# The context's Fourier mixing ahead of the experts, and the rest of layer 0's modulation right behind the router

## Chip, cores and metric

The kernel runs on one core of a Trainium2 chip. The metric is the device time of one execution, in microseconds (us). A measurement is the median of several executions.

## What is computed

Two transformer blocks, one behind the other, on 256 tokens of width 1024, all in float32. The first mixes tokens (two kinds of attention), attends to a memory of 256 rows, and has a mixture of 16 experts. The second has two layers that work on two streams: the latent `x` (what the first block gives) and a context of 256 rows, which doesn't depend on the first block. The part of the reference that the change touches:

```python
mod_c = jax.nn.silu(c_ctx) @ w_mod[l] + b_mod[l]      # and mod from c
sh1c, sc1c, ga1c, sh2c, sc2c, ga2c = jnp.split(mod_c, 6, axis=-1)
hc = modulate(rmsnorm(xc, g_norm1[l]), sh1c, sc1c)
pfc, mqc, mkc, mvc, moc, mgc, cqc, ckvc, krc = split_proj(hc @ w_in[l])
...
y_fc = fourier_mix(pfc)          # real part of a 2-d FFT per group of 64
y_mc = mlstm_output(hcf, hcb, moc, g_mlstm[l])
y_ac = merge_heads(softmax_attend(qn_c, qr_c, (ctx_keys,)))
xc = xc + ga1c * (jnp.concatenate([y_fc, y_mc, y_ac], axis=-1) @ w_out[l])
xc = xc + ga2c * sqrelu_mlp(modulate(rmsnorm(xc, g_norm2[l]), sh2c, sc2c), w_up[l], w_down[l])
```

The modulation vectors of a layer depend on `c`, `c_ctx` and `w_mod` alone, so they can be computed at any time before their use.

## The kernel before

**Products.** A float32 product is made from three products of rounded parts: each weight tile is loaded (`raw`), ACT casts its high part (`whi`, L330), DVE subtracts it from the tile (`wlo`, L331), and PE adds up hi x hi, lo x hi and hi x lo (L364 to L366, in `gemm_a`). Activations are split in the same way: `th`/`tl` for a norm's output, `x2h`/`x2l` for the mixed heads that the output projection of a layer takes in, `hh`/`hl` inside the MLP. `wload` does this, with buffers of their own for work in the foreground and in the background.

**Order.** The program is written as a chain of regions, each with a rank from a table (`RK`): first 10, context in 19, experts 20, context out 22, context mix 23, and so on. A scheduler lists each engine's instructions ahead of time: an instruction of lower rank goes first where it is ready by the scheduler's own model, and one of a higher rank fills in. The engines then take their rows strictly in that order. All weight loads are on SP's queue.

**Layers.** `Layer(l, s)` is one layer of the second block on a stream (s = 1: context). `norm1` is its first norm, `enter` makes keys, queries, values and gates, `gate_out` and `spectrum_in` two more input products, `recur` the mLSTM (L962 to L1020, scores and their weights, one step for each of four heads), `attend` the attention (L919 scores, L928 transposes of the weights, L932 the sum over values, L936/L937 its scale, L942 the transposes of the result), `fourier` the Fourier mixing: four products with a table `dft` (L889), a copy (`z`), and eight with `cn` and `sn` (L898, L899), a split into `x2h`/`x2l` for the first two of eight rows of the projection. `project` is the projection, `norm2` and `mlp` follow. A norm sums squares (L419), takes a root on POOL, makes a diagonal tile `dg` (L433 on DVE, L431 on ACT), spreads it with a product (L435), and then scales each of eight tiles (`nt`, L454; `tl`, L464). The latent's first norm in layer 0 folds in the first block's last norm: its sums are L616 to L627, it has two diagonal tiles and two L435, the second for the residual (L635).

**Modulation.** `w_mod` of both layers is done in 48 rounds (`mod_jobs`, three groups of eight rounds for each layer). A round loads two tiles of 512 KB (L526) into two buffers and runs four matmuls side by side (L538); each waits for both loads. After eight rounds a sum (`modulate_sum`, four products L554, then L555, and L561 where a gain is folded in) gives 16 columns of modulation. `modulation(l, f)` runs all that is still to do up to column group f; `spread(3, 0, 47)` lets `tick` give one step with every third weight load of the foreground. Before the change the main program spreads the rounds over the first block, and the rest of layer 0 comes with the weight loads of the latent's `enter`, or at the latest where `project` and `norm2` of the context ask for it.

**The branch.** Behind the experts the kernel tests whether a group of experts overflowed (`experts_over`, L1635). The order of each engine is cut there: rows ahead of the branch, and rows behind it.

**Main program around the change** (L1660 on): `mix_tokens`, the context's `context_in` (rank 19, background), `mix_memory` (memory attention, and the router at L1352 to L1359), `context_mix` (rank 23, background), then `experts`, `experts_over`, and the latent's layer 0.

```python
    def context_mix(L):
        L.recur()
        L.attend()
        L.fourier()
```

Of the kernel before, what the change touches and what calls it, by code (L numbers as in the profile page):

```python
# [222 lines left out]
def _body(ctx, tc, A, out):  # L223
# [343 lines left out]
    def pending(l, f):  # L567
        return "done" in part or mod_jobs and mod_jobs[0] <= (l, f // 16, KT - 1)

    def modulation_step():  # L570
        with background(True):
            if "done" in part:
                modulate_sum()
            else:
                modulate_round(*mod_jobs.pop(0))

    def modulation(l, f):

        while pending(l, f):
            modulation_step()  # L580

    def spread(every, l, f):

        pace[0], pace[1], pace[2] = every, (l, f), 0
# [520 lines left out]
    def load_ctx():  # L1105
        RES[1] = [slot(256, name="ctx") for _ in range(KT)]
        for k in range(KT):
            nc.sync.dma_start(RES[1][k], A["ctxT"][:, k, :])

    def context_in():  # L1110
        load_ctx()
        L = Layer(0, 1)
        L.norm1()
        L.enter()
        L.gate_out()
        L.spectrum_in()
        L.share()
        return L

    def context_mix(L):  # L1120
        L.recur()
        L.attend()
        L.fourier()

    def context_out(L):
        load_ctx()
# [486 lines left out]
    def experts(R):  # L1613
        U, SN, gate, _ = R
        ready = {}

        def prepare(q):
            O = dispatch(SN, q)
            ready[q] = gather(U, O), slot_gates(O, gate, q), [back(O, p) for p in range(2)]
        prepare(0)  # L1620
        for p in range(8):
            q = p // 2
            if q not in ready:
                prepare(q)
            us, W, OT = ready[q]
            j = p % 2
            pair_experts([u[:, j * 128:(j + 1) * 128] for u in us], W[:, j:j + 1], OT[j], p)
            if p % 2 == 0 and q < 3:
                prepare(q + 1)
# [33 lines left out]
    with region(RK["ctx"], True):  # L1663
        LC = context_in()
    with region(RK["first"]):
        XG = mix_memory()
    with region(RK["cmix"], True):
        context_mix(LC)
    with region(RK["moe"]):
        spread(0, 0, 0)  # L1670
        experts(XG)
        experts_over(XG)
        spread(3, 0, 47)
        L = Layer(0, 0)
# [17 lines left out]
    with region(RK["l1"]):  # L1692
        L = Layer(1, 0)
# [47 lines left out]
```

## Time and profile before

| | us |
|---|---|
| median of 3 runs | 1589.96 |
| lowest and highest | 1586.74 and 1597.65 |
| the profiled execution | 1601.72 |
| its span in the profile | 1599.6 |

The profile is of one execution. PE is TensorE, PEld its weight loads, DVE the vector engine, ACT the scalar engine, POOL GpSimd, SP the engine that issues the loads. Times count from the start of the span. A matmul on float32 data (Fourier, modulation, attention) appears as two records, the products of rounded parts as one. A row of a timeline names the line of the code, the operation, what it writes and reads, and in brackets how long the engine was idle before it and what it waited for.

### The profile page before, as it was taken

To read this page: it belongs to the slowest core of one execution; us is meant where nothing else is said; L and a number is where in the kernel's file an instruction comes from. 1 tells how busy PE (TensorE), PEld (TensorE's weight loads), DVE (VectorE), ACT (ScalarE), POOL (GpSimd) and SP (SyncE) were. 2 spreads that over 40 slices of the span, in tenths; PEclk is the share of its full clock that TensorE was granted. 3 is DMA by queue.
4 is the path that set the end of the run, shared out by engine and by line. 5 is a ranking of instruction groups with operands and counts; after the bars stand their busy time and mean duration, and the time that the engine had idled before them with its cause. 6 is when DMAs were issued, how large, how long until landed. Compare 5 with 4: busy or idle time off the path is not lost. (4 is left out here: it accounts for less than half of the span.)

```text
span 1599.6 us, 27409 instructions
## 1 busy us (share of the span) xinstructions
PE 1514.9 (95%) x10646; PEld 1298.3 (81%) x10646; DVE 911.7 (57%) x1937; ACT 711.2 (44%) x1530; POOL 30.2 (2%) x99
## 2 busy tenths in 40 slices
PE   6999999989999986999999999999999899999998
PEld 5669788867744445888998999999888677899998
DVE  5635466676633437675675434444776663576665
ACT  4435555444422234465554323233545445455555
POOL 0000000000000000000000000000000000000000
PEclk9869999999999997999999999999989998999999
DMA  7735554354678765432355422222356651245553
GB/s 245 255 132 186 183 184 171 136 211 158 219 252 295 277 236 186 159 120 69 102 197 217 146 92 95 91 95 95 123 172 247 215 202 43 102 145 176 187 183 119
DMA packets 91001, 268.65 MB, mean 168 GB/s; under 512 B 10224, under 2 KB 16368, under 8 KB 90864
## 3 DMA queue, kind: packets, MB, share of 16 engines
q1 hardware_dynamic: 90864, 266.83, 47.8%
q8 instruction: 86, 1.41, 0.3%
q14 instruction: 51, 0.42, 0.1%
HBM read 265.74 MB, written 1.05 MB: 167 GB/s over the span
## 5 line engine op out<-in xcount | busy, mean ns | idle before, releaser
L330 ACT CAST whi<-raw 128x512 fp32r<-128x512 f32 (+2 forms) x614 | 364.0, 602 | 449.3 <-PE ps L365 360.6
L331 DVE TENSOR_TENSOR wlo<-raw,whi 128x512 fp32r<-128x512 f32 (+2 forms) x614 | 404.4, 668 | 275.8 <-ACT whi L330 268.2
L364 PE MATMUL ps<-th,whi 128*128 128x256 f32 x1496 | 433.8, 291 | 4.4 <-ACT th L463 3.2
L366 PE MATMUL ps<-th,wlo 128*128 128x256 f32 x1496 | 427.7, 287 | 5.2 <-DVE wlo L331 5.2
L365 PE MATMUL ps<-tl,whi 128*128 128x256 f32 x1496 | 429.3, 289 | 0.1
L364 PEld LDWEIGHTS ps<-th,whi 128*128 128x128 f32 x1496 | 289.7, 194 | 21.4 <-ACT th L463 5.4
L366 PEld LDWEIGHTS ps<-th,wlo 128*128 128x128 f32 x1496 | 289.1, 194 | 9.5 <-DVE wlo L331 7.5
L365 PEld LDWEIGHTS ps<-tl,whi 128*128 128x128 f32 x1496 | 289.1, 194 | 7.9 <-issue 5.0
L364 PE MATMUL ps<-hh,whi 128*128 128x256 f32 x768 | 218.0, 284 | 2.1 <-ACT hh L474 1.0
L365 PE MATMUL ps<-hl,whi 128*128 128x256 f32 x768 | 217.0, 283 | 0.2 <-DVE hl L475 0.2
L366 PE MATMUL ps<-hh,wlo 128*128 128x256 f32 x768 | 216.9, 283 | 0.0
L364 PEld LDWEIGHTS ps<-hh,whi 128*128 128x128 f32 x768 | 145.2, 189 | 4.8 <-ACT hh L474 2.7
L365 PEld LDWEIGHTS ps<-hl,whi 128*128 128x128 f32 x768 | 144.3, 188 | 0.5 <-DVE hl L475 0.5
L366 PEld LDWEIGHTS ps<-hh,wlo 128*128 128x128 f32 x768 | 144.2, 188 | 0.3
L538 PE MATMUL mod<-raw,scT 128*32 128x512 f32 x320 | 67.1, 644 | 8.6 <-DMA raw<-in_wmod_dram 8.5
L1552 PE MATMUL ps<-raw,us 128*64 128x512 f32 x128 | 59.4, 601 | 1.0 <-DMA raw<-in_wgu_dram 0.9
L364 PE MATMUL ps<-x2h,whi 128*128 128x256 f32 x192 | 55.0, 286 | 0.5 <-ACT x2h L474 0.5
L366 PE MATMUL ps<-x2h,wlo 128*128 128x256 f32 x192 | 54.6, 284 | 0.4 <-DVE wlo L331 0.4
L365 PE MATMUL ps<-x2l,whi 128*128 128x256 f32 x192 | 54.6, 284 | 0.1
L1064 DVE SCALAR_TENSOR_TENSOR res<-ps,mod,res 128x256 f32<-128x256 f32 x80 | 35.1, 479 | 33.2 <-PE ps L366 33.1
L1094 DVE TENSOR_TENSOR rl<-rl 128x512 f32<-128x512 f32 x48 | 32.9, 686 | 34.5 <-ACT rl L1092 34.5
L395 PE MATMUL ps<-whi,th 128*128 128x512 f32 (+1 forms) x128 | 48.4, 382 | 0.1
(416 smaller groups left out, 2224.3 us busy)
## 6 DMA issues: line engine op xcount, KB each, us to landing
raw<-in_wmod_dram SPq DMA_DIRECT2D x80, 512.0 KB, 4.6
raw<-in_wup_dram SPq DMA_DIRECT2D x72, 512.0 KB, 3.2
raw<-in_wdn_dram SPq DMA_DIRECT2D x64, 512.0 KB, 3.2
raw<-in_wo_dram SPq DMA_DIRECT2D x32, 512.0 KB, 3.2
raw<-in_wgu_dram SPq DMA_DIRECT2D x32, 512.0 KB, 4.6
raw<-in_w2m_dram SPq DMA_DIRECT2D x29, 512.0 KB, 3.4
raw<-in_w2c_dram SPq DMA_DIRECT2D x21, 512.0 KB, 3.5
raw<-in_w1a_dram SPq DMA_DIRECT2D x16, 512.0 KB, 4.5
```

The lines of the kernel that those rows point to most:

```text
L330: nc.scalar.copy(hi, raw[:, p * m:p * m + m])
L331: nc.vector.tensor_sub(lo, raw[:, p * m:p * m + m], hi)
L364: mm(o, wh, xh, start=k == order[0] and not (both and j), stop=False)
L365: mm(o, wh, xl, start=False, stop=False)
L366: mm(o, wl, xh, start=False, stop=k == order[-1] and (not both or j == len(fs) - 1))
L395: mm(o, xh, wh, start=st, stop=False)
L538: m = mm(ps[32 * j:32 * j + 32, :], scT[:, k, :], W[j], start=k == 0, stop=k == KT - 1, tile_position=(0, 32 * j))
L1064: stt(self.res[f], ps[:, j * 256:(j + 1) * 256], self.mod[:, off + f, self.s:self.s + 1], self.res[f], op0=ALU.mult, op1=ALU.add)
L1094: tt(r_, r_, r_, op=ALU.mult)
L1552: mm(ps[64 * j:64 * j + 64, :], us[k][:, 64 * j:64 * j + 64], ws[j][kk], start=k == 0, stop=k == 7, tile_position=(0, 64 * j))
```

## The change

`fourier` of the context moves from `context_mix` (behind recurrence and attention, rank 23) into `context_in` (ahead of `share`, rank 19). And behind `mix_memory`, in the region of rank 10, the main program asks for all of layer 0's modulation.

```diff
@@ -1114,13 +1114,13 @@
         L.enter()
         L.gate_out()
         L.spectrum_in()
+        L.fourier()
         L.share()
         return L
 
     def context_mix(L):
         L.recur()
         L.attend()
-        L.fourier()
 
     def context_out(L):
         load_ctx()
@@ -1664,6 +1664,7 @@
         LC = context_in()
     with region(RK["first"]):
         XG = mix_memory()
+        modulation(0, 47)
     with region(RK["cmix"], True):
         context_mix(LC)
     with region(RK["moe"]):
```

PE, the first rows behind the branch. `ya` is the context's attention, `wq` the squares' weights of the latent's first norm, `mod` a round of modulation; L364 on `th` is the first product of the latent's layer. Before:

```order
L942 MATMUL ps<-cst,ya 128x128
L621 MATMUL ps<-wq,sq 128x2 x2
L942 MATMUL ps<-cst,ya 128x128
L621 MATMUL ps<-wq,sq 128x2 x2
L942 MATMUL ps<-cst,ya 128x128
L621 MATMUL ps<-wq,sq 128x2 x12
L942 MATMUL ps<-cst,ya 128x128 x2
L435 MATMUL ps<-dg,cst 128x256
L538 MATMUL mod<-raw,scT 32x512
L435 MATMUL ps<-dg,cst 128x256
L364 MATMUL ps<-th,whi 128x256
```

After the change:

```order
L621 MATMUL ps<-wq,sq 128x2 x16
L928 MATMUL ps<-cst,ae 128x128 x2
L932 MATMUL pa<-vm,apt 128x96 x2
L435 MATMUL ps<-dg,cst 128x256
L942 MATMUL ps<-cst,ya 128x128 x6
L364 MATMUL ps<-x2h,whi 128x256
L365 MATMUL ps<-x2l,whi 128x256
L366 MATMUL ps<-x2h,wlo 128x256
L364 MATMUL ps<-x2h,whi 128x256
```

The round has gone from behind the branch. The end of the context's attention (L928, L932) has come there from ahead of it, and 13 rows of the context's projection (L364 to L366 on `x2h`/`x2l`) stand between the two L435.

SP, ahead of the router: the weights of memory attention (`wxq`, `wxv`, `wxo`), of the context (`w2m`, `wuv`, `wuq`) and of the modulation (`wmod`). Before:

```order
L324 DMA raw<-in_wxq_dram 128x1024 x5
L324 DMA raw<-in_wxv_dram 128x1024 x2
L324 DMA raw<-in_wxq_dram 128x1024
L324 DMA raw<-in_w2m_dram 128x1024
L324 DMA raw<-in_wxq_dram 128x1024 x2
L324 DMA raw<-in_wxo_dram 128x1024 x5
L324 DMA raw<-in_w2m_dram 128x1024 x2
L810 DMA wuv<-in_wukv_dram 128x384
L836 DMA wuq<-in_wuq_dram 128x512 x2
L526 DMA raw<-in_wmod_dram 128x1024 x2
L324 DMA raw<-in_w2m_dram 128x1024
```

After the change:

```order
L324 DMA raw<-in_wxq_dram 128x1024 x4
L526 DMA raw<-in_wmod_dram 128x1024
L324 DMA raw<-in_wxq_dram 128x1024
L526 DMA raw<-in_wmod_dram 128x1024
L324 DMA raw<-in_wxv_dram 128x1024 x2
L526 DMA raw<-in_wmod_dram 128x1024
L324 DMA raw<-in_wxq_dram 128x1024 x3
L324 DMA raw<-in_wxo_dram 128x1024 x5
L526 DMA raw<-in_wmod_dram 128x1024
L324 DMA raw<-in_w2m_dram 128x1024 x2
L526 DMA raw<-in_wmod_dram 128x1024 x2
L324 DMA raw<-in_w2m_dram 128x1024
```

Loads of the modulation now stand singly between those of memory attention, from the queries' weights on.

PE, in the third step of the latent's recurrence. Before, the last three of ten rows of the context's projection stand ahead of the first product with `mw`:

```order
L366 MATMUL ps<-x2h,wlo 128x256
L364 MATMUL ps<-x2h,whi 128x256
L365 MATMUL ps<-x2l,whi 128x256
L366 MATMUL ps<-x2h,wlo 128x256
L998 MATMUL ps<-vr,mw 128x97
L364 MATMUL ps<-x2h,whi 128x256
L962 MATMUL ps<-qkc 128x256 x2
L968 MATMUL ps<-grr,selr 128x512
L970 LDWEIGHTS bfc
L970 MATMUL ps<-bfc 128x256
L998 MATMUL ps<-state,qx 128x97
```

After the change, at the same step:

```order
L968 MATMUL ps<-grr,selr 128x512
L970 LDWEIGHTS bfc
L970 MATMUL ps<-bfc 128x256
L419 MATMUL ps<-cst,sq 128x1 x4
L998 MATMUL ps<-vr,mw 128x97
L962 MATMUL ps<-qkc 128x256 x2
L968 MATMUL ps<-grr,selr 128x512
L970 LDWEIGHTS bfc
L970 MATMUL ps<-bfc 128x256
```

The rows of the projection are gone from there; the sum of the context's second norm (L419) has taken their place.

## Rows read from the trace of the kernel before

**Rows 1.** The page, part 1: busy us (share of the span) and instructions.

```profile
PE 1514.9 (95%) x10646; PEld 1298.3 (81%) x10646; DVE 911.7 (57%) x1937; ACT 711.2 (44%) x1530; POOL 30.2 (2%) x99
```

**Rows 2.** Stretches: length, busy PE, PEld, DVE, ACT, POOL, PEclk, DMA, GB/s.

```profile
300.00:592.00 292.00, 274.86 (x1660) 178.59 (x1662) 155.21 (x412) 101.63 (x261) 7.40 (x26) 0.98 0.67 233
440.00:560.00 120.00, 113.44 (x607) 58.41 (x607) 48.34 (x131) 30.00 (x92) 1.98 (x2) 0.99 0.78 275
595.00:615.00 20.00, 9.85 (x40) 8.27 (x41) 9.59 (x26) 9.36 (x23) 2.26 (x6) 0.50 0.56 197
617.00:629.00 12.00, 12.00 (x95) 11.82 (x95) 10.35 (x23) 6.40 (x12) 0.00 (x0) 0.93 0.28 95
629.00:639.00 10.00, 6.21 (x37) 4.55 (x35) 8.05 (x21) 5.97 (x12) 0.95 (x8) 0.84 0.61 209
639.00:643.00 4.00, 4.00 (x21) 3.92 (x20) 1.15 (x2) 0.62 (x1) 0.00 (x0) 0.54 0.22 85
643.00:665.00 22.00, 20.79 (x144) 18.48 (x144) 16.75 (x39) 10.33 (x25) 0.76 (x2) 1.00 0.47 156
680.00:740.00 60.00, 58.86 (x441) 53.14 (x440) 43.85 (x104) 36.76 (x100) 2.55 (x7) 1.00 0.29 100
740.00:770.00 30.00, 27.24 (x179) 24.23 (x178) 15.90 (x35) 16.04 (x36) 0.70 (x1) 0.94 0.16 53
```

**Rows 3.** PE behind the branch: start, us, instruction, [idle before <-releaser].

```profile
595.18 0.45 PE L942 MATMUL ps<-cst,ya 128*128 128x128 f32 x1 [2.37 <-PEq L1635]
...
614.65 1.91 PE L538 MATMUL mod<-raw,scT 128*32 128x512 f32 x2 [7.53 <-DMA raw<-in_wmod_dram]
...
616.56 1.19 PE L435 MATMUL ps<-dg,cst 128*128 128x256 f32 x2
```

**Rows 4.** Timeline of DVE in the first hole.

```profile
603.75 0.41 DVE L475 TENSOR_TENSOR x2l<-ps,x2h 128x256 fp32r<-128x256 f32 x1
...
609.33 0.68 DVE L331 TENSOR_TENSOR wlo<-raw,whi 128x512 fp32r<-128x512 f32 x1
...
616.13 0.28 DVE L433 TENSOR_SCALAR dg<-cst,rp 128x128 f32<-128x128 f32 x1
```

**Rows 5.** Timeline of PE in the second hole.

```profile
629.53 1.06 PE L538 MATMUL mod<-raw,scT 128*32 128x512 f32 x6
...
630.52 1.99 PE L889 MATMUL ps<-dft,pf 128*128 128x256 f32 x8
...
632.35 0.95 PE L554 MATMUL mod<-cst,mrow 128*128 128x8 f32 x8
...
638.07 1.22 PE L435 MATMUL ps<-dg,cst 128*128 128x256 f32 x2 [2.63 <-ACT dg L431]
```

**Rows 6.** Timeline of PE in the Fourier's second half.

```profile
652.00 0.59 PE L899 MATMUL ps<-sn,z 128*128 128x256 f32 x2
652.43 0.59 PE L898 MATMUL ps<-cn,z 128*128 128x256 f32 x2
```

**Rows 7.** PE by line, 300 to 592 us: busy, mean ns of one, idle.

```profile
L932 PE MATMUL pa<-vm,apt 128*128 128x96 f32 x32 | 5.3, 287 | 2.4 <-ACT apt L930 2.4
...
L928 PE MATMUL ps<-cst,ae 128*128 128x128 f32 x16 | 3.4, 297 | 0.0
```

**Rows 8.** Waits of PE, 300 to 592 us: in total, times, longest.

```profile
PE ps L968 <- ACT mw L976: 2.7, 4, 0.9
PE ps L1569 <- ACT ht L1562: 2.5, 5, 0.6
PE pa L932 <- ACT apt L930: 2.4, 5, 0.5
```

**Rows 9.** Timeline of SP's queue ahead of the branch.

```profile
579.70 13.48 SPq L526 DMA_DIRECT2D raw<-in_wmod_dram  x3
```

**Rows 10.** Timeline of PE at the context's second norm.

```profile
757.41 0.70 PE L435 MATMUL ps<-dg,cst 128*128 128x256 f32 x2 [1.46 <-ACT dg L431]
...
759.22 0.58 PE L364 MATMUL ps<-th,whi 128*128 128x256 f32 x1 [1.11 <-ACT th L463]
```

## Prediction

> **What bounds the kernel now.** I read the page's first lines, then busy time by stretches, then each engine's instructions around the places that the change touches. The whole says that TensorE leads: PE is busy 95% of the span [rows 1]. An average hides where time can be won, so the stretches come next [rows 2]. Between 300 and 592 us (memory attention's end, router, experts) PE is busy 274.86 of 292 us, and in the experts, 440 to 560, 113.44 of 120: work added there costs nearly its own length. Behind the branch that follows the experts it is otherwise: 9.85 of 20 us in 595 to 615 and 6.21 of 10 in 629 to 639. These two holes are norms, the latent's first one and the one of its keys. From 680 to 740, in the recurrence, PE is full again (58.86 of 60), because the context's output projection lies ready as filler.
>
> The holes row by row. In the first, PE leaves the branch at 595.18 after 2.37 us, and at 614.65 a round of modulation starts after 7.53 us, named as a wait for its weights' DMA [rows 3]. That name misleads: the second L435 behind it, which the first layer product needs for the residual's scale, multiplies a tile that DVE begins only at 616.13 (0.28 us) [rows 4], so it could not have run before about 616.4 and ran at 616.56. The hole is a chain on DVE, and taking the DMA wait away gives some 0.15 us. The second hole is the 8.5 us from 629.53 to 638.07 [rows 5]: the last three matmuls of the round, half of the Fourier mixing (L889), the modulation's sum (L554), then 2.63 us idle before the keys' L435.
>
> So the end is set by PE, and the time is its work plus its holes. The change moves work over the branch; the total of work stays. Only what fills a hole counts.
>
> **The change part by part.** The sum is made against the profiled execution, 1601.72 us (span 1599.6). The median of the runs is 1589.96, 11.8 us below it, so I carry the difference over to the median.
>
> 1. *Ahead of the branch.* The four L889 come in: 1.99 us [rows 5]. The eight L898/L899: two stand 0.43 us apart (652.00 and 652.43) [rows 6], 3.4 us together. Of modulation one round (three of its four matmuls, which run side by side, take 1.06 in rows 5; I take 1.1) and one sum (0.95) more: layer 0's rounds all end behind the router instead of in the experts and beyond, which for those that only move from the experts to the router's stage changes nothing. Out goes the end of the context's attention: two transposes L928, two L932 (two passes each) and one L942, 0.30 and 0.29 us a piece [rows 7] and 0.45 at the low clock [rows 3], 2.2 us added up but overlapping; I take 1.3. That is 5.4 + 1.1 + 0.95 - 1.3 = +6.1. The waits that a filler could take are small: 2.5 us in five places before L1569 and 2.4 in five before L932 [rows 8], and Fourier's products meet one or two of them. I take +5.5; bounds +3 (every such wait met) and +8 (the Fourier's casts on ACT and DVE delay the experts' by 2 us).
>
> The extra loads (one round, the three Fourier tables) lie beside a DMA share of 0.78 in 440 to 560 [rows 2]: no cost, as long as the rows under "rivals" do not go wrong. SP held its queue 13.48 us at 579.70 with three modulation loads [rows 9]; after the change nothing stands there. No engine needs SP until the weights of the first gemm, 25 us later: 0.
>
> 2. *First hole.* Its DVE chain loses nothing and gets three x2l of the attention's end between the norm's tl tiles (0.41 us each [rows 4]): +1.2; the L942 that stood among the L621 in before (0.45 each, overlapping) no longer do: -0.5. So +0.7 (bounds 0, +1.5). What fills it instead of the round are 13 matmuls of the context's projection ("X2" below, 192 in all) and six L942.
>
> 3. *Second hole.* One more wlo (0.68 [rows 4]) and two residual updates of the context (128 x 256, taken at the 0.41 of an x2l) come before the keys' scale on DVE: +1.5 (bounds 0, +2.5). Fourier, round and sum leave it, and 37 X2 enter; a full stretch of the same matmuls, 617 to 629, has 95 in 12 us [rows 2], and as a few records can be missing I take 0.12 us each: 4.4 us, which fit.
>
> 4. *Up to the queries' norm.* L898/L899 leave (3.4), as do 0.7 us of idle around the first X2, and 116 X2 stand there instead of 61: 55 x 0.12 = 6.5. So +2.3 (bounds +1, +4).
>
> At the queries' norm the changed kernel is then 5.5 + 0.7 + 1.5 + 2.3 = 10.0 us late, but 105 X2 ahead, worth 12.4: -2.4 net.
>
> 5. *Recurrence and attention.* 131 X2 were left there as filler; now 26 are. The context's second norm and its MLP take their place, and the last three heads of the recurrence, which had 45 X2 between their steps, have almost none. What an uncovered step costs is not seen behind the branch; the nearest row is the context's own recurrence in the experts, where L968 waits 2.7 us for mw in four heads with other work around [rows 8]. Three heads at 0.7 us: +2 (bounds 0 and +4).
>
> 6. *The context's second norm.* In before it stands alone in the attention and leaves PE idle 1.46 and 1.11 us [rows 10], and the granted clock of 740 to 770 is 0.94 [rows 2], 0.06 x 30 = 1.8 us at half speed, some 0.9 us lost. Moved into the recurrence, it lies beside that chain: -3.5 (bounds 0, -4).
>
> 7. *Clock.* The granted clock is 0.50 (1.2 of 2.4 GHz) in 595 to 615, where PE was idle half of the time, and 0.54 in 639 to 643, right behind the second hole [rows 2]. The second hole now holds more work; half of what those 4 us lose (about 1.9): -1 (bounds -2, 0). The first stays cold.
>
> Sum: -2.4 + 2 - 3.5 - 1 = -4.9 us. Predicted: 1589.96 - 4.9 = 1585.
>
> **Rivals.**
>
> *The experts absorb it (faster).* If the experts' PE had room, item 1 would be 0 and the sum -10.4, 1579.6. For it: weight loading is busy only 58.41 of 120 us there. Against it: the matmul rows fill 113.44 of 120 [rows 2]. The Trainium skill's page "Perfetto Trace Analysis" (Identifying the Most-Contended Engine) holds matmul busy time for a poor measure, since matmuls are pipelined, and wants the weight-load share read instead; by that rule there is room, by the busy rows there is not. Matmul rows that follow one another with 6 us of idle time in 120 leave little place for others, so I keep them. With items 5 to 7 at their good ends as well it would be -16, 1574.
>
> *A late round blocks PE (slower).* Layer 0's rounds now stand earlier, among the loads of the queries' and output weights of memory attention. PE takes its rows in order, and the round at 614.65 shows what a late one costs: 7.53 us [rows 3], and SP stands just as long behind a load whose buffer is not free (13.48 us [rows 9]). Two of the moved rounds late, or a weight load held behind them, is +15 before the router, where nothing covers it: -4.9 + 15 = +10, 1600. It decides from the point where a round's load lands later than its turn on PE; against it stands that the modulation's two buffers leave a round's time for the load.
>
> *DVE becomes the bound (no gain).* The 105 X2 that come earlier bring about nine more casts to wlo (0.68 us) into 595 to 665, where DVE is already busy 8.05 of 10 us in the second hole and 16.75 of 22 behind it [rows 2]. If they all land on the norms' chains, items 2 and 3 grow by 4 us and, with the recurrence uncovered (+4 in place of +2) and no gain from the norm, the sum is -4.9 + 4 + 2 + 3.5 = +4.6, 1594.6.
>
> *It does not do what it says.* The holes are made by DVE chains, not by missing filler; then what fills them is taken from later filler one for one, and all is within 2 us of 0.
>
> **How the numbers follow.** The forecast case has 0.4 (1578 to 1593 from its bounds), absorption 0.2, DVE or nothing won 0.25, the late round 0.15. A measurement of this kernel tells about 1%, 16 us, from no change. Faster by over 1% (below 1574) needs absorption with all good ends, or more than my bounds of the holes: half of absorption and some of the forecast, 0.18. Slower by over 1% (above 1606) needs two or three late rounds, or two rivals together: 0.14. Within 1%: 0.68. The range is 1572 to 1602: it takes in both rivals' ends and leaves out most of the late rounds and of the best case.
>
> **What would show it.** The branch leaves about 5.5 us later (PE's first row behind it near 600.7 by the profile's time); holes of the same length behind it, with X2 matmuls and no L538, L889 or L554 in them; the queries' norm about 10 us later than before; idle time between L968 and L998 in the recurrence that was not there; no wait of 1 us and more at the context's second norm; from layer 0's second norm of the latent on, 5 us earlier. Wrong would be: a wait for a modulation load ahead of the router, experts that end less than 3 us or more than 8 us later, or a recurrence that loses more than 4 us.

## The result, and the profile after

The changed kernel takes 1603.95 us (median of 20 runs, 1595.64 to 1616.53), the kernel before 1591.81 in the same series (20 runs, 1581.48 to 1610.01). The ratio is 1.007, with a 95% interval of 1.0049 to 1.0091: a loss of 0.7%, 11 us, where a gain of 0.3% was forecast. The time lies just above the range given.

The profiled execution of the changed kernel is 1604.12 us, that of before 1601.72. They are only 2.4 us apart because a single execution moves by several us in places where both kernels run the same rows in the same order, with another granted clock: up to 210 us the order on TensorE is identical, and yet executions of these kernels reach that place between 200 and 215 us. So no time from the start of the span is compared here, but stages between marks that are the same instruction in each kernel:

- A: the first transposes L1225 of the second attention's output (214.7 us before, 210.0 after);
- M: the L435 of the context's first norm (the one whose tiles L463 shifts by `mod`; it stands behind memory attention's third group of scores L1315, and one expectation below calls it the memory's norm); R: the router's first L1359, its third product; E: the experts' first product L1552; P: the last product L1528 that puts the experts' rows back; Q: the first product on the latent's queries; N: the latent's second norm in layer 0.

The stages before, by those marks (A to M, M to R, R to E, E to P, P to Q, Q to N; columns: length, busy PE, PEld, DVE, ACT, POOL, granted PE clock, DMA share, GB/s):

```profile
214.70:290.30 75.60, 75.40 (x531) 68.34 (x532) 47.74 (x93) 40.69 (x83) 1.40 (x2) 1.00 0.48 168
290.30:348.80 58.50, 52.69 (x372) 46.59 (x371) 38.98 (x89) 27.39 (x64) 2.47 (x6) 0.94 0.48 168
348.80:379.20 30.40, 28.37 (x210) 22.92 (x210) 25.25 (x97) 13.20 (x31) 1.35 (x8) 0.94 0.35 124
379.20:591.40 212.20, 201.86 (x1114) 115.96 (x1114) 97.65 (x245) 65.26 (x177) 3.59 (x12) 0.99 0.74 260
591.40:673.80 82.40, 65.06 (x393) 56.62 (x392) 55.34 (x130) 38.41 (x83) 4.10 (x16) 0.81 0.47 162
673.80:843.30 169.50, 163.83 (x1224) 150.58 (x1222) 114.09 (x253) 92.77 (x222) 3.25 (x8) 0.99 0.38 129
```

The same six stages of the changed kernel, and behind them its two holes behind the branch, which answer to [rows 2]:

```profile
210.00:295.10 85.10, 83.18 (x564) 70.17 (x565) 48.68 (x98) 42.21 (x87) 1.39 (x2) 0.99 0.56 183
295.10:350.50 55.40, 50.00 (x364) 43.69 (x363) 38.02 (x81) 26.02 (x59) 2.03 (x6) 0.95 0.56 198
350.50:387.70 37.20, 32.23 (x221) 29.05 (x220) 26.91 (x103) 13.62 (x31) 0.94 (x8) 0.80 0.32 105
387.70:601.50 213.80, 201.90 (x1117) 120.00 (x1117) 97.92 (x244) 67.35 (x180) 3.59 (x12) 1.00 0.72 251
601.50:688.90 87.40, 71.46 (x456) 67.31 (x455) 62.35 (x143) 42.59 (x92) 4.21 (x16) 0.80 0.45 142
688.90:851.60 162.70, 156.51 (x1120) 141.54 (x1119) 104.75 (x237) 85.95 (x210) 2.72 (x8) 0.96 0.38 124
...
606.10:624.00 17.90, 11.12 (x46) 9.64 (x46) 9.18 (x25) 8.98 (x25) 1.98 (x4) 0.50 0.53 173
628.00:650.00 22.00, 18.21 (x141) 17.65 (x140) 19.57 (x45) 13.27 (x25) 0.95 (x8) 0.89 0.37 125
```

Read the first column. A to E is 164.5 us before and 177.7 after: 13.2 us lost ahead of the experts. E to P takes 1.5 more: the Fourier mixing has come into it, and four groups of modulation matmuls have left it. P to Q takes 5.0 more and Q to N 6.9 less. A to N together is 12.9 us longer, which agrees with the 11 us of the ratio. From N to the end both kernels run the same order; there executions of that order take 750 to 760 us (756.3 before, 750.6 after), so nothing is read from that part.

The whole says nothing of this; PE's line on the page answers to [rows 1] and is 4 us less, in an execution that is 2.4 us longer:

```profile
PE 1510.8 (94%) x10646; PEld 1298.0 (81%) x10646; DVE 911.9 (57%) x1937; ACT 710.9 (44%) x1530; POOL 29.0 (2%) x99
```

**Ahead of the router.** The modulation rounds on PE between A and M in the changed kernel (start, us, instruction; two records are one matmul on float32 data):

```profile
214.19 1.04 PE L538 MATMUL mod<-raw,scT 128*32 128x512 f32 x2
...
235.49 1.06 PE L538 MATMUL mod<-raw,scT 128*32 128x512 f32 x6
...
245.88 1.05 PE L538 MATMUL mod<-raw,scT 128*32 128x512 f32 x2
...
250.14 1.05 PE L538 MATMUL mod<-raw,scT 128*32 128x512 f32 x4
...
271.05 1.04 PE L538 MATMUL mod<-raw,scT 128*32 128x512 f32 x2
...
276.84 1.04 PE L538 MATMUL mod<-raw,scT 128*32 128x512 f32 x2
...
281.47 1.06 PE L538 MATMUL mod<-raw,scT 128*32 128x512 f32 x6
...
290.17 1.06 PE L538 MATMUL mod<-raw,scT 128*32 128x512 f32 x8
```

A round is four matmuls, eight records. Three of the four rounds here are torn into two or three groups with other rows between, and a group lasts 1.04 to 1.07 us whether one matmul is in it or four (the next product starts 0.97 to 1.00 us behind it). So these four rounds are eight groups, where before had one round in two groups. Six groups at 0.98, one sum L554 (the next product starts 0.80 us behind its start) and 1.7 us of idle time at L1331 are 8.4 of the 9.5 us by which A to M grew; PE was busy there 75.40 of 75.60 us before, so there was no idle time to take them.

**Between router and experts.** PE at the norm of the context's keys, after the change:

```profile
355.50 0.37 PE L714 MATMUL ps<-cst,gst 104*128 104x104 f32 x2 [0.55 <-DVE gst L698]
356.72 0.29 PE L718 MATMUL ps<-cst,gsx 40*128 40x40 f32 x2 [0.85 <-DVE gsx L704]
356.94 1.06 PE L538 MATMUL mod<-raw,scT 128*32 128x512 f32 x8
...
358.85 1.78 PE L554 MATMUL mod<-cst,mrow 128*128 128x8 f32 x8 [0.22 <-ACT mrow L547]
...
360.48 0.99 PE L419 MATMUL ps<-cst,acc 128*128 128x1 f32 x4
363.00 1.22 PE L435 MATMUL ps<-dg,cst 128*128 128x256 f32 x2 [1.53 <-ACT dg L431]
...
368.14 2.25 PE L1464 MATMUL ps<-identr,th 128*128 128x128 f32 x16
```

and before:

```profile
355.50 0.66 PE L419 MATMUL ps<-cst,acc 128*128 128x1 f32 x4
356.09 1.92 PE L538 MATMUL mod<-raw,scT 128*32 128x512 f32 x4
358.10 1.22 PE L435 MATMUL ps<-dg,cst 128*128 128x256 f32 x2
...
362.76 1.53 PE L1464 MATMUL ps<-identr,th 128*128 128x128 f32 x16
```

Before, a piece of a round stood between L419 and L435 and covered the norm's chain. Now the last round comes earlier (356.94, between two other waits), a sum stands ahead of L419, the norm waits 1.53 us, and PE stays at half clock longer: the same sixteen L1464 take 2.25 us in place of 1.53, and R to E has a granted clock of 0.80 in place of 0.94. Of the 6.8 us by which R to E grew, 2.9 are idle time (4.97 for 2.03) and 3.9 busy time (32.23 for 28.37), which holds the sum and the half-clock rows.

**Behind the branch.** PE's rows with a wait (and the L942 between them) in the changed kernel, which answer to [rows 3, 5, 10]:

```profile
606.11 6.96 PE L621 MATMUL ps<-wq,sq 128*128 128x2 f32 x32 [4.19 <-ACT sq L619]
...
615.94 1.06 PE L942 MATMUL ps<-cst,ya 128*128 128x128 f32 x4
623.00 0.69 PE L942 MATMUL ps<-cst,ya 128*128 128x128 f32 x2 [6.00 <-DVE x2l L475]
...
644.62 0.37 PE L714 MATMUL ps<-cst,gst 104*128 104x104 f32 x2 [1.95 <-DVE gst L698]
...
649.77 1.22 PE L435 MATMUL ps<-dg,cst 128*128 128x256 f32 x2 [1.46 <-ACT dg L431]
...
744.87 2.04 PE L919 MATMUL ps<-kT,qT 96*128 96x256 f32 x4 [1.36 <-DVE mw L981]
```

No L538, L889 or L554 stands there, as the prediction said, and the first hole still has a wait of 6.00 us, now named as one for x2l: it was the norm's chain, not the round. The new row is the last, at the end of the recurrence. The stretches around it:

```profile
720.00:730.00 10.00, 10.00 (x77) 8.96 (x76) 6.25 (x16) 6.29 (x20) 0.00 (x0) 1.00 0.52 170
730.00:740.00 10.00, 9.28 (x40) 6.33 (x39) 3.59 (x12) 4.48 (x16) 0.70 (x1) 0.72 0.00 0
740.00:750.00 10.00, 8.64 (x42) 7.44 (x42) 5.53 (x16) 4.80 (x16) 0.00 (x0) 0.60 0.01 2
```

PE reads as busy 9.28 and 8.64 of 10 us, but with half as many instructions as the 77 of the stretch above, at a granted clock of 0.72 and 0.60. In before the recurrence ran at 1.00 [rows 2].

### The profile page after: what moved, and what is told of

It is laid out like the page before. It is cut to its first block, busy times and chain, and to the rows that moved or that the text cites. A ratio compares the mean times of both kernels' runs of the same rounds, so it can differ in the third digit from the quotient of the medians.

```text
span 1602.2 us, 27415 instructions
## 1 busy us (share of the span) xinstructions
PE 1510.8 (94%) x10646; PEld 1298.0 (81%) x10646; DVE 911.9 (57%) x1937; ACT 710.9 (44%) x1530; POOL 29.0 (2%) x99
## 5 line engine op out<-in xcount | busy, mean ns | idle before, releaser
L364 PE MATMUL ps<-th,whi 128*128 128x256 f32 x1496 | 432.8, 291 | 4.1 <-DVE qrs L859 1.3
L366 PE MATMUL ps<-th,wlo 128*128 128x256 f32 x1496 | 426.9, 286 | 5.6 <-DVE wlo L331 5.6
L364 PEld LDWEIGHTS ps<-th,whi 128*128 128x128 f32 x1496 | 288.7, 194 | 23.0 <-issue 5.8
L366 PEld LDWEIGHTS ps<-th,wlo 128*128 128x128 f32 x1496 | 287.9, 193 | 10.3 <-DVE wlo L331 7.6
L364 PE MATMUL ps<-hh,whi 128*128 128x256 f32 x768 | 218.7, 285 | 1.2 <-ACT whi L330 0.4
L366 PE MATMUL ps<-hh,wlo 128*128 128x256 f32 x768 | 216.6, 282 | 0.0
L364 PEld LDWEIGHTS ps<-hh,whi 128*128 128x128 f32 x768 | 144.8, 189 | 3.3 <-ACT hh L474 1.7
L366 PEld LDWEIGHTS ps<-hh,wlo 128*128 128x128 f32 x768 | 144.7, 189 | 0.3 <-DVE wlo L331 0.2
L538 PE MATMUL mod<-raw,scT 128*32 128x512 f32 x320 | 61.1, 624 | 0.9 <-DMA raw<-in_wmod_dram 0.9
L1552 PE MATMUL ps<-raw,us 128*64 128x512 f32 x128 | 60.5, 608 | 0.6 <-DMA raw<-in_wgu_dram 0.4
L366 PE MATMUL ps<-x2h,wlo 128*128 128x256 f32 x192 | 55.3, 288 | 0.8 <-DVE wlo L331 0.8
L364 PE MATMUL ps<-x2h,whi 128*128 128x256 f32 x192 | 55.6, 289 | 0.4 <-DVE x2l L475 0.4
L1064 DVE SCALAR_TENSOR_TENSOR res<-ps,mod,res 128x256 f32<-128x256 f32 x80 | 35.0, 479 | 33.1 <-PE ps L366 33.1
```

The source lines that it names most:

```text
L364: mm(o, wh, xh, start=k == order[0] and not (both and j), stop=False)
L366: mm(o, wl, xh, start=False, stop=k == order[-1] and (not both or j == len(fs) - 1))
L538: m = mm(ps[32 * j:32 * j + 32, :], scT[:, k, :], W[j], start=k == 0, stop=k == KT - 1, tile_position=(0, 32 * j))
L1064: stt(self.res[f], ps[:, j * 256:(j + 1) * 256], self.mod[:, off + f, self.s:self.s + 1], self.res[f], op0=ALU.mult, op1=ALU.add)
L1552: mm(ps[64 * j:64 * j + 64, :], us[k][:, 64 * j:64 * j + 64], ws[j][kk], start=k == 0, stop=k == 7, tile_position=(0, 64 * j))
```

## The experiments

Thirteen kernels were run. The table gives each one's stages as differences to before (us, one profiled execution each) and the ratio of the timed runs. How far a stage repeats can be read where two kernels have the same order: A to M agrees within 0.1 us, but P to N lies between -1.3 and -5.4 in five kernels whose rows behind P are the same (after, mod19, half5, late_sum, spread2). A to N agrees with the ratio (times 1592 us) within 3 us in nine of the fourteen rows, within some 7 in mod19, after_whole and cmix195; in spread2 and mod21_whole 9 to 10 us of the difference lie outside A to N. In spread2 and after_whole about two rounds more than before stand ahead of A, and a sum; in the last three rows the rounds ahead of A and behind N are also packed in fewer groups.

| | A to E | E to P | P to Q | Q to N | A to N | ratio to before |
|---|---|---|---|---|---|---|
| before (length) | 164.5 | 212.3 | 82.4 | 169.5 | 628.7 | |
| after | +13.2 | +1.5 | +5.0 | -6.9 | +12.9 | 1.007 [1.0049, 1.0091] |
| fourier_only | -0.7 | +5.3 | +8.7 | -20.1 | -6.7 | 0.9959 [0.9927, 0.9991] |
| mod_only | +12.0 | -2.7 | -0.2 | -5.2 | +3.9 | 1.001 [0.9973, 1.0047] |
| mod21 | -0.6 | +5.0 | +9.6 | -19.7 | -5.6 | 0.995 [0.9914, 0.9985] |
| mod19 | +0.9 | +7.0 | +3.8 | -9.2 | +2.4 | 0.9978 [0.9948, 1.0009] |
| half5 | +8.8 | +5.7 | +3.7 | -5.9 | +12.3 | 1.006 [1.0025, 1.0095] |
| late_sum | +8.7 | +4.3 | +3.4 | -5.3 | +11.2 | 1.0078 [1.0047, 1.0109] |
| spread2 | +13.3 | -0.1 | +3.9 | -5.2 | +12.0 | 1.0136 [1.009, 1.0181] |
| hold3 | +12.6 | +0.4 | +3.6 | -2.4 | +14.3 | 1.0075 [1.0042, 1.0108] |
| fourier_hold | -0.1 | +3.6 | +5.5 | -8.7 | +0.3 | 1.0004 [0.9965, 1.0043] |
| cmix195 | +14.0 | +21.9 | +7.0 | -25.1 | +17.9 | 1.0068 [1.0035, 1.0101] |
| before_whole | -6.8 | -4.2 | -1.6 | -4.4 | -17.0 | 0.9897 [0.9851, 0.9944] |
| after_whole | +8.7 | -1.7 | +4.8 | -7.4 | +4.4 | 0.9995 [0.9961, 1.0028] |
| mod21_whole | -6.5 | +2.8 | +3.9 | -7.0 | -6.8 | 0.9902 [0.9872, 0.9931] |

**The two halves apart.** fourier_only takes the main program's new line out:

```diff
         XG = mix_memory()
-        modulation(0, 47)
```

> Only the Fourier mixing moves; the modulation stays as before. Theory A (two losses: rounds and a sum crowded in at the router, some 5 us; and a recurrence of the latent's layer that runs out of the projection's matmuls, some 8 us against the forecast): the router loss is gone, so the first expert product starts within 2 us of before (379 us), the branch comes some 5 us late by the Fourier's own work, and the recurrence still lacks filler with a granted clock under 0.9 there; ratio to before 1.002 to 1.005. Rival B (the Fourier's 5.4 us in the full experts are the loss and never come back): about as slow as the whole change, 1.006 to 1.008.

mod_only puts the Fourier mixing back:

```diff
         L.spectrum_in()
-        L.fourier()
         L.share()
...
         L.attend()
+        L.fourier()
```

> Only the modulation is asked for behind the router; the Fourier mixing stays behind the attention. Theory A: the router loss shows alone, the first expert product is 5 to 9 us late with a granted clock near half right before it, while the projection still waits for the Fourier mixing so that most of its matmuls remain for the recurrence; ratio 1.001 to 1.005. Rival B (all of the loss is the Fourier's): 1.000 or below.

The Fourier mixing alone is a gain of 0.4%, which neither theory of its expectation had; the modulation alone is no change that can be told, though it delays the first expert product by 12.0 us, more than the 5 to 9 expected. The Fourier costs 4.6 us from A to P, near its own length, and gives 11.4 back behind. The modulation costs 12.0 from A to E and the experts give back 2.7 of it. Ahead of the branch the two add up (4.6 + 9.3 = 13.9, measured 14.8). Behind it they do not: -11.4 and -5.4 alone, -1.9 together.

**The modulation's place.** Three kernels keep the change and move the new line's rank:

```diff
         XG = mix_memory()
+    with region(19.2, True):
         modulation(0, 47)
```

is mod19; mod21 has 21 in its place, behind the experts' own rows (20); half5 asks for five rounds in the foreground and gives the rest rank 21:

```diff
+        for _ in range(5):
+            modulation_step()
+    with region(21, True):
         modulation(0, 47)
```

> The whole change with the modulation asked for at the context's rank (19.2, background) instead of the foreground's: up to the router the order is that of before, the last three rounds and the sum come between the router and the second pair of experts, and behind the branch the order is word for word that of the whole change. Theory E: the loss behind the branch stays, what goes is the crowding ahead of the router: ratio 1.003 to 1.006. Rival F (all of the loss stands at the router): 0.998 or below, like the Fourier mixing alone.

> The Fourier mixing moved, and the modulation asked for behind the router, but at rank 21, behind the experts' own: up to the branch the order is that of the Fourier mixing alone; the last round and the sum come into the first hole, between the projection's matmuls, instead of the second. Theory E: as fast as the Fourier mixing alone or up to 3 us faster, 0.993 to 0.997. Rival G (a round and a sum between the projection's matmuls hold up the norm's second root): slower than that, 0.998 to 1.001.

> The whole change, but only five of layer 0's remaining modulation steps at the foreground's rank behind memory attention, the others as before and at rank 21; behind the branch the order is that of the whole change. Theory I (the cost goes by the rounds moved ahead of the experts): about half of the 10 us that the whole change loses up to the branch against the Fourier mixing alone come back, ratio 1.001 to 1.005. Theory H (it is the last sum and round at the context's key norm): nearly all of it comes back, 0.996 to 1.001.

In mod19 the order of PE behind the branch is that of the changed kernel, word for word, the program has as many groups of L538 (57; before has 60), and no further round is pulled ahead of M: A to E falls from +13.2 to +0.9, the experts, which now hold two rounds and the sum, take 5.4 more, and the ratio falls from 1.007 to 0.9978. The intervals don't touch. That is the ratio of its rival F, though what theory E says of the part behind the branch stays true: the recurrence (below) is 4.5 us longer than before here too. So the place of the rounds ahead of the experts makes the loss, at an equal number of groups. mod21 has fourier_only's stages and 0.995. half5 has 58 records of L538 between A and E, where before has 42 and the changed kernel 72; but ahead of M it has the same eight groups and the sum as the changed kernel. A to E falls to +8.8, the experts take 4.1 more for it, and nearly all of the loss stays: 1.006, outside both ranges expected.

late_sum leaves the rounds where the change puts them and holds the last sum (L554) until the first pair of experts is through, as an order alone (the sum is asked for at rank 20.5 for that):

```diff
+            if (l, f) == (0, 32):
+                tc.add_manual_dep(m.ins, state["pair"].ins.name, ...)
...
-        modulation(0, 47)
+        while mod_jobs[0][0] == 0:
+            modulation_step()
...
+    with region(20.5, True):
+        modulation(0, 47)
```

> The whole change, but the last modulation sum (four narrow matmuls and what follows) may not come before the last product of the first pair of experts; the rounds stay ahead of the router. Theory H (at the router the sum stands ahead of the context's key norm, delays it and lets the clock fall, some 4 us of the loss): from the last common row to the first expert product 3 to 5 us shorter than the whole change, with the granted clock of the 10 us before and behind the norm over 0.7 instead of 0.5; ratio 1.003 to 1.006. Rival I (it is the rounds as such: each in the full stage costs its 1.06 us and more): within 1 us of the whole change there, 1.006 to 1.008.

It takes 4.4 us off R to E, as its theory H has it, but not by taking a wait away:

```profile
351.20:384.05 32.85, 27.97 (x213) 24.98 (x213) 26.08 (x101) 13.78 (x32) 0.94 (x8) 0.90 0.34 117
```

PE is idle 4.9 us there, as in the changed kernel, and the key norm's L435 still waits 1.53. What goes is the sum's own time and time at half clock (granted 0.90 instead of 0.80). And it gains nothing: the experts take 2.8 us more, and the ratio stays, as the rival has it. spread2 gives a modulation step with every second weight load of the first block instead of every third:

```diff
-        spread(3, 0, 47)
+        spread(2, 0, 47)
```

> The whole change, but the rounds come with every second weight load of the first block instead of every third, so that layer 0's are through before the router and none stands in it. Theory A: the first expert product starts no more than 2 us after that of before, and 3 to 6 us of the loss come back: ratio 1.003 to 1.005. Rival D (the extra loads ahead of the router compete with the weights of the first block): as slow as the whole change or slower, 1.007 to 1.012.

That is worse than the change, 1.0136, and above both ranges expected. A to M alone is 21.4 us longer than before (9.5 with the change) and M to R gives 10.2 back; what makes it worse than the change lies outside A to N, and which rows it is was not followed.

**The filler of the recurrence.** hold3 holds part of the context's projection (from the fourth of its eight column blocks on, an order only) until the latent's last input product, so that the recurrence has filler again; fourier_hold holds all of the projection, without the modulation, until the latent's first norm is through; cmix195 gives the context's mixing rank 19.5, so that it ends ahead of the branch:

```diff
+                if state.get("hold") and f0 + j >= 3:
+                    for m in ms:
+                        tc.add_manual_dep(m.ins, state["hold"].ins.name, ...)
```

```diff
-"cout": 22, "cmix": 23,
+"cout": 22, "cmix": 19.5,
```

> The whole change, but from the fourth of eight column blocks on, the matmuls of the context's output projection may not come before the latent's last input product (an order on the engine alone, no new wait elsewhere). Theory A: the recurrence has filler again, its granted clock is 1.00, and most of the 8 us come back: ratio to before 1.000 to 1.003. Rival C (what the recurrence lost was given back elsewhere, or the loss is in the holes and the experts): 1.006 to 1.008, as the whole change.

> The Fourier mixing alone moved, and the projection's matmuls may not come before the second root product of the latent's first norm (an order on the engine alone): up to the branch the order is that of the Fourier mixing alone (0.996), the first hole loses its 67 projection matmuls, and the context's second norm falls into the recurrence. Theory E: 8 to 13 us of its gain go, ratio 1.001 to 1.005. Rival F (order behind the branch does not matter, the router's does): 0.995 to 0.998, as without the hold.

> The whole change with the rank of the context's recurrence and attention at 19.5 instead of 23, so that the attention ends ahead of the branch: up to the router the order is that of the whole change; behind the branch 51 of the projection's matmuls stand in the first hole (13 in the whole change), and the context's second norm comes around the queries' norm instead of into the recurrence. Theory E (the changed kernel loses because the projection starts too late behind the branch, so that the gap between projection and MLP falls into the recurrence): the stretch from the queries to the latent's second norm shortens by 8 us or more against the whole change; ratio 0.998 to 1.003. Rival F (the loss is what stands at the router): 1.005 to 1.009 as before.

hold3 does to the recurrence what it was meant to. The last 20 us of its recurrence:

```profile
708.00:718.00 10.00, 10.00 (x75) 8.79 (x75) 5.71 (x15) 6.85 (x21) 0.00 (x0) 1.00 0.44 143
718.00:728.00 10.00, 10.00 (x69) 8.04 (x68) 6.94 (x18) 6.35 (x21) 0.00 (x0) 1.00 0.18 64
```

The clock is 1.00 again and the stage that holds the recurrence (scores L962 to the latent's first L919, 27.7 us before) is 1.1 us shorter than before, where the changed kernel's is 5.4 longer. Yet Q to N gains less, and the ratio is that of the changed kernel, as rival C has it: filler that is held for one gap is missing in another. fourier_hold shows the same from the other side: holding costs 11.4 us of Q to N, and the gain of 0.4% is gone (1.0004, between the two ranges expected). cmix195 takes 25.1 us out of Q to N, and the experts, which have to carry the work, pay 21.9 of it; its ratio is that of rival F.

In fourier_only the context's attention ends ahead of the branch, so its projection starts in the first hole with 67 matmuls where the changed kernel has 13, and the sums of the context's second norm stand beside the queries' norm. The last 20 us of its recurrence, which runs from 703.7 to 730.3:

```profile
710.00:720.00 10.00, 10.00 (x77) 9.01 (x76) 9.30 (x26) 8.34 (x25) 0.00 (x0) 1.00 0.11 33
720.00:730.00 10.00, 10.00 (x68) 8.02 (x68) 7.28 (x18) 6.66 (x22) 0.00 (x0) 1.00 0.37 127
```

All 192 matmuls of the projection stand ahead of the queries there, none is left for the recurrence, and yet it is 1.2 us shorter than before. The second norm's L435 stands in its first step (705.81), so products of the context's MLP can fill the steps behind it; in the changed kernel that L435 stands at the recurrence's end (742.40). In all seven kernels that leave 26 of them, with the sums of the second norm some 21 us into the recurrence (after, mod19, half5, late_sum, spread2, after_whole, mod21_whole), it is 4.1 to 6.0 us longer. So the loss goes with the place of the second norm, and not simply with the number of projection matmuls left.

**The price of a torn round.** Three kernels keep the four L538 of every round, in both layers, in adjacent rows: matmuls two to four of a round get the first rank and an order behind the first.

```diff
         for j in range(4):
+            rank = tc.cur_priority
+            if j:
+                tc.cur_priority = 0
             m = mm(ps[32 * j:32 * j + 32, :], scT[:, k, :], W[j], ...)
+            if j:
+                tc.cur_priority = rank
+                tc.add_manual_dep(m.ins, first.ins.name, ...)
+            else:
+                first = m
```

before_whole, after_whole and mod21_whole are before, the change and mod21 with this edit.

> The kernel before, with the four matmuls L538 of each modulation round kept in adjacent rows of TensorE (order only, all rounds of both layers). Groups of L538 in its order: 41 instead of 60 (ahead of the router's product 19 instead of 26, from there to the experts 1 instead of 3, in the experts 4 instead of 5, behind the branch none instead of 2, later 17 instead of 24). Theory 'a group costs 1.05 us whatever is in it': 19 x 1.05 = 20 us where TensorE is full, of which I expect half to show: the ratio to the kernel before 0.987 to 0.996; each L538 group x8 near 1.06 us. Rival 'a round costs by its matmuls, split or not': within 0.003 of 1. Rival 'place decides': also within 0.003 of 1, since the places are nearly the same.

> The changed kernel with the same edit. Groups of L538: 41 instead of 57; from the first block's attention to the router's product 7 instead of 12, none between router and experts instead of 1. Theory 'price by group': the loss against the kernel before shrinks from 1.007 to 0.993 to 1.001, and the stretch from the second attention's output to the memory's norm costs +3 to +6 us over the kernel before instead of +9.5. Rival 'place decides' (rounds ahead of the experts meet full stretches and the router's waits, however they are packed): it stays 6 us or more over before_whole, and its stretch from the router to the first expert keeps a good part of its +6.8 us. Both can hold: the group price shows in after_whole against the changed kernel, the place in after_whole against before_whole.

> The changed kernel with the remaining modulation of layer 0 at rank 21, behind the experts' own rows instead of ahead of them (as in the run mod21), and with the four matmuls of a round in adjacent rows. It differs from after_whole only in where the rounds stand, and from before_whole only by the Fourier mixing ahead of the branch. Price by group: 18 groups fewer than mod21, ratio 0.983 to 0.992. Rival 'by matmuls': as mod21, 0.995 within 0.003. Place: after_whole is 8 to 15 us slower than this one.

All three gain, each within the range expected of the price by group: 1.0% (19 groups fewer in the program), 0.75% (16 fewer, 1.007 to 0.9995) and 0.5% (18 fewer, 0.995 to 0.9902). That is 8 to 16 us, between 0.4 and 0.9 us for a group; the 0.5% of mod21_whole is not clear of the noise, since its interval overlaps that of mod21. That a round pays by its groups and not by its matmuls is therefore the better account. The edit moves other rows as well (in all three the end of the context's attention falls behind the branch, and in the first hole mod21_whole has 13 matmuls of the projection, as the changed kernel, where mod21 has 72), so not each of these us is a group's. And the stretch from A to M, for which 3 to 6 us were expected, is +11.6 in after_whole: two rounds more than in the changed kernel and more of the context's rows came into it, and M to R is 12.5 shorter for it.

The place counts beside the packing: after_whole is 1.0% (16 us) behind before_whole, with the same 41 groups. Its stages A to M, M to R and R to E:

```profile
210.50:297.70 87.20, 85.30 (x595) 72.92 (x595) 51.97 (x102) 43.52 (x92) 1.39 (x2) 1.00 0.63 220
297.70:343.70 46.00, 41.55 (x310) 38.41 (x311) 32.77 (x74) 23.90 (x53) 2.08 (x6) 0.96 0.48 165
343.70:383.70 40.00, 32.36 (x225) 29.89 (x223) 28.62 (x105) 14.35 (x32) 0.94 (x8) 0.81 0.21 67
```

and those of before_whole:

```profile
196.60:266.00 69.40, 68.60 (x505) 63.54 (x505) 44.53 (x88) 38.23 (x79) 1.78 (x2) 1.00 0.49 170
266.00:327.30 61.30, 57.40 (x408) 51.04 (x409) 48.40 (x116) 30.98 (x74) 3.18 (x14) 0.94 0.54 184
327.30:354.20 26.90, 23.89 (x194) 20.81 (x191) 21.21 (x83) 11.92 (x27) 0.00 (x0) 1.00 0.30 104
```

R to E is 40.0 against 26.9 us, but it does not hold the same work: the key norm's L435 stands ahead of R in before_whole (324.60) and behind it in after_whole (356.73). All three stages together are 173.2 against 157.6 us, with PE idle 14.0 us against 7.7, two rounds more (16 records of L538), and in R to E a clock of 0.81 against 1.00. In before_whole a round stands just ahead of the key norm's L435 (322.74) and another among the places' waits (342.95); in after_whole the last round is at 326.86, ahead of the router, and the norm waits 2.3 us uncovered. mod21_whole, whose rounds stand as in before_whole, is level with before_whole: 0.9902 against 0.9897. Against after_whole it is some 15 us faster, as mod19 is against the changed kernel: both pairs have equal numbers of groups and differ in the place of the rounds. With whole rounds the Fourier mixing ahead of the experts wins nothing that can be told any more; the context's attention ends behind the branch there, and Q to N gives back 7.0 us where mod21 gave 19.7. By the ratios, before_whole and mod21_whole are 1% faster than before and 1.7% faster than the changed kernel.

## Why the prediction was wrong

*Item 1, ahead of the branch: +5.5 forecast, +14.8 measured (A to P); 9.3 of the miss.* The Fourier's part was right: 5.4 less 1.3 priced, 4.6 measured in fourier_only. The step that failed is the sentence on the rounds "which for those that only move from the experts to the router's stage changes nothing". It failed in two ways that the runs part:

- A round was priced as 1.06 us. The unit is the group, and [rows 5] had shown it: three matmuls in one group at 1.06. Ahead of M the rounds are torn, six more groups: about 6 us there, of which M to E saves two again. The `whole` runs show the price of tearing. But the changed kernel has three groups fewer than before in the whole program (57 for 60), so tearing does not make the net loss: before tears its rounds too, in stages that have room.
- They moved further than to the router's stage: four rounds and a sum stand ahead of M, and A to M was full (75.40 of 75.60 us). Between router and experts, where three pieces of rounds had stood in and beside the waits, PE is idle longer and at half clock longer. That is the +6.8 of R to E, of which late_sum moved 4.4 and kept nothing. mod19 against the changed kernel shows the price of the place at equal groups, some 15 us by the ratios, and mod21_whole against after_whole shows it without the tearing, some 15 us as well.

The experts gave the moved groups back at about their price: the Fourier's 5.3 less 1.5 is 3.8 us for four groups (2.7 in mod_only). That is what "changes nothing" rested on, and it is less than what they cost ahead. A whole round (1.07 us) that stood between P and the branch before also moved ahead of P; so about 1 us of the 9.3 is no loss up to the branch, and P to Q hides as much. The prediction's own sign of being wrong, experts that end more than 8 us later, came true.

*Items 2 to 4 and 7, the holes up to the queries: +4.5 - 1 = +3.5 forecast, +5.0 measured (P to Q); 1.5 of the miss.* The holes are as described: up to the second L435 +0.4 (+0.7 forecast), from there to the keys' L435 +1.2 (+1.5), from there to the queries +3.4 (+2.3, bound 4). Item 7 did not come: in the 4 us behind the keys' L435 the granted clock was 0.50 (650.7 to 654.7), where before had 0.54.

*Items 5 and 6 and the 105 matmuls that come earlier (-12.4 + 2 - 3.5 = -13.9 forecast; -6.9 measured, Q to N): 7.0 of the miss.* Item 5 was mis-sized: the recurrence cost not 2 us but 6.9 (1.5 up to its scores, 5.4 to L919), above its bound of 4, because the clock falls with it (0.84 from scores to L919, 1.00 before) and the context's second norm lies in the same place; idle time is the smaller part (3.4 us up to L919, against 0.16 x 33.1 = 5.3 us of lost clock). What failed in it is "the context's second norm and its MLP take their place": the norm stands there (sums from 732.30, L435 at 742.40), and the MLP behind it comes too late. What remains lies behind the recurrence, -13.8 measured for -12.4 - 3.5 = -15.9: 2.1 us, which fit item 6, but no run parts them. hold3 shows that the recurrence was the place, and also that filling it again only opens the next gap; which fits a lack of filler as a whole, and no edit tried here with the rounds in their changed place regained it. That both items fail together only when rounds and Fourier move together (-11.4 and -5.4 alone, -1.9 together) is seen; which rows make the difference in each case was followed only for the projection's matmuls and the norm, so the cause of that part stays open in the rest. At 4 us of spread between kernels of one order, the smaller terms here are not parted from noise.

The sum closes: -4.9 + 9.3 + 1.5 + 7.0 = +12.9, the stages' own total.

*Its arithmetic.* Three figures in the prediction do not follow from its terms. Absorption with items 5 to 7 at their good ends is -10.4 - 2 - 0.5 - 1 = -13.9, not -16. The bounds added up give 1575.6 to 1597.6, not 1578 to 1593. And a clock of 0.94 over 30 us loses 0.06 x 30 = 1.8 us, as item 7 reckons it, not half of that. None of them moves the forecast nearer to what was measured.

*The rivals.* The experts did not absorb the Fourier mixing: E to P grew by 5.3 us in fourier_only, though weight loading is busy only 115.96 of 212.20 us in that stage. The Trainium skill's page "Perfetto Trace Analysis" (Identifying the Most-Contended Engine) judges TensorE's headroom by MFU (the matmul work done over the peak) and the weight-load share, and not by matmul busy time. The weight-load share, the one of the two that was read here, pointed the wrong way. The late round came to pass in size (1600 forecast by it), but not in kind: no L538 of layer 0 ahead of the router waits for its load in the changed kernel. DVE did not become the bound in the holes (items 2 and 3 came out below their forecast). "It doesn't do what it says" was half true: the first hole is as long without the round as with it (25.4 us from P to the second L435, 25.0 before), with a wait of 6.00 us in it.

## What to carry to other kernels

Filler is worth what the gap it fills is worth, once. Before moving it forward, look at the stage it will be pulled to (is the engine full there?) and at the one it leaves (which chain did it cover?); this scheduler took the first place that its model called free, 60 us and more ahead of the router. And price small matmuls that run side by side by the group: keep the members of a group in adjacent rows, and count how many groups an order makes of them.

## Hardware behaviour that was not expected

A group of L538 (128x512, 32 columns of weights each) lasts 1.04 to 1.07 us at a granted clock of 1.00 with one, two, three or four matmuls in it, and the next product starts 0.97 to 1.00 us behind its start. At half clock it is 1.91 and 1.92 us for one matmul ([rows 3]) and for two (356.09 before).

A stretch in which the busy rows of PE fill 86 to 93% can still have a granted clock of 0.60 to 0.72 (730 to 750 us after the change); what stands there are mostly small products of the recurrence (L998, L968, L962), 40 and 42 instructions against 77 at a clock of 1.00. PE's busy share alone hides such a loss; the count of instructions and the granted clock beside it show it. The router shows the same: sixteen L1464 take 2.25 us where they took 1.53, right behind a norm in which PE had waited several times.
